# A second block product per group in the MLPs of a two-layer trunk: seven products in place of eight for all columns, alternating with the first layer

## The chip, the cores and the metric

The kernel runs on one core of a Trainium2 chip. The metric is the time of one execution on the device in microseconds (us), the median of three runs. A profiled execution is a further one, with its own time. Engines: TensorE (PE, with its weight loads PEld), VectorE (DVE), ScalarE (ACT), GpSimd (POOL), SyncE (SP). Each takes its instructions in the order in which the build wrote them.

## The reference, cut to what matters

256 tokens of width 2048 pass through two layers. Each has a recurrent mixer and a dense MLP with a hidden width of 8192, both between RMS norms, and a residual add. Only the MLP is touched:

```python
def sqrelu_mlp(h, w_up, w_down):
    u = jax.nn.relu(h @ w_up)
    return (u * u) @ w_down

f = sqrelu_mlp(rmsnorm(h, norm_mlp_pre[i]), mlp_w_up[i], mlp_w_down[i])
h = h + rmsnorm(f, norm_mlp_post[i])
```

`h` in the last line is the residual stream, 256 x 2048 in float32. Everything is float32. The kernel gets near that precision by splitting each operand into a rounded part (hi) and the rest (lo) and adding three products: hi·hi, hi·lo, lo·hi.

## The kernel before

**Splitting.** A weight block is 128 partitions x 2048 float32, 1 MiB. SP loads it into one of three `raw` tiles. It is split by halves of 1024 columns: ScalarE writes hi (`split_hi`, L103), VectorE writes lo = raw - hi (`split_lo`, L107), each into one of five buffers.

**First layer** (`up`, L526). The hidden width is taken in 8 groups of 1024, each of 8 blocks of 128. One block is one *first-layer product* (`gemmT`, L148): 16 matmuls of 512 columns (both parts of the activations against hi) and 16 of 256 (against lo), into one bank. It is folded (`fold`: ScalarE copies one half, VectorE adds), made relu and squared, and split into hi and lo of `U`.

**Second layer.** For a group, 1024 hidden rows meet 4 column blocks of 512 (n = 0 to 3) for two token tiles (t = 0, 1). In *plain* form (`plain`, L644) one column block takes 2 x 8 x 3 = 48 matmuls of 512. For n = 0, 1 the kernel treats the product as a 2 x 2 block matrix product (token tile x half of the hidden rows, times half x column block) and uses seven products in place of eight, after Strassen and Winograd (`seven`, L595). One of the seven takes 4 x 3 = 12 matmuls of 512. Four of them use sums of activation blocks, which VectorE forms (`combine`, L514); weights are summed too. Writing B11, B21 for the two halves of the hidden rows at the first column block and B12, B22 at the second, these are the weight sums:

- the *run* tile (pool `sump`, one buffer): first B11 + B12, then B22 is added, then B21. Adding is done by an accumulating DMA that POOL issues (`add_to`, L571).
- the *q* tiles (pool `accp`, two halves, one buffer): B12 + B22.

After each product VectorE adds the bank to, or takes it from, the sums `m[n, t]` (`put`, L588).

**Order.** Emission order is that of the generators `up`, `seven` and `plain`. All of a group's first-layer products are emitted, then `down` mixes the seven products of that group with the plain ones of the group before. A build-time scheduler then moves instructions somewhat, engine by engine; what it wrote is fixed.

The residual `h` lies in SBUF throughout (L55), 2 MiB.

## Time and profile before

| | |
|---|---|
| median of 3 runs | 2280.74 us (2280.22 to 2281.78) |
| profiled execution, its own time | 2281.16 us |
| its span, first to last instruction | 2279.4 us |
| mean granted TensorE clock | 0.999 |
| span of the first MLP, about | 447 to 1121 us |
| span of the second MLP, about | 1683 to 2279 us |
| HBM read | 513.47 MB |

The page gives the busy time of each engine, then groups of instructions. Matmuls overlap, so the pace of TensorE is read from the starts of its instructions. "Landing" of a DMA is the time from its issue until its data is there. The releaser in brackets is what ended an engine's idle time.

### The profile page before, as it was taken

The numbers are of one execution on the slowest core, as the hardware profiler recorded it, in microseconds if no ns is written. First come the engines' busy times: TensorE is split into PE (matmuls) and PEld (weight loads), VectorE is DVE, ScalarE is ACT, GpSimd is POOL, SyncE is SP. The second block draws the span as 40 slices with busy tenths as digits, with TensorE's granted clock in tenths as the row PEclk, the third lists the DMA queues.
The fourth block names the chain that finished last, engine by engine and source line by source line (L and its number), as shares of the span: only waits on it lengthen the run. The fifth ranks groups of instructions, "written<-read, shape, count | busy, mean of one in ns | idle before, by whom it ended". The sixth has DMA issues, their size and how long they took to land.

```text
span 2279.4 us, 30175 instructions
## 1 busy us (share of the span) xinstructions
PE 2263.6 (99%) x11528; PEld 1925.7 (84%) x11528; DVE 1719.5 (75%) x2575; ACT 1330.1 (58%) x1919; POOL 69.6 (3%) x84
## 2 busy tenths in 40 slices
PE   9999999999999999999999999999999999999998
PEld 7888888888888888888888887888888888888887
DVE  6887877667778778778786767656787877877877
ACT  7555554556555556555567456555665555555654
POOL 0000000000000000000000000000000000000000
PEclk9999999999999999999999999999999999999999
DMA  8544545558888788788764544465789878878875
GB/s 330 169 165 165 177 156 185 173 196 260 271 289 261 247 262 267 247 277 255 244 222 150 202 166 149 166 208 184 248 269 310 249 247 279 249 247 277 255 246 162
DMA packets 82288, 517.52 MB, mean 227 GB/s; under 512 B 9792, under 2 KB 10176, under 8 KB 25696
## 3 DMA queue, kind: packets, MB, share of 16 engines
q1 hardware_dynamic: 70480, 448.23, 54.2%
q0 software_dynamic: 11520, 67.11, 15.5%
q8 instruction: 90, 1.47, 0.3%
q14 instruction: 54, 0.44, 0.1%
q10 hardware_dynamic: 144, 0.26, 0.0%
HBM read 513.47 MB, written 2.10 MB: 226 GB/s over the span
## 4 chain that ended last, share of the span: by engine, by line
PE 93%; DVE 3%; DMA 2%; ACT 1%; issue 0%; SPq 0%; DVEq 0%; ACTq 0%
PE mmT L155 26%; PE mmT L158 14%; PE mm L137 12%; PE mm L136 12%; PE mm L135 12%; PE sa L620 7%; PE sb L620 3%; PE sc L620 2%; PE sc L758 2%; DVE lo L107 1%; DMA bs<-w_dn 1%; DMA raw<-w_dn 1%; PE tr L191 1%; DVE xhl L204 1%; PE sd L793 0%
## 5 line engine op out<-in xcount | busy, mean ns | idle before, releaser
L107 DVE TENSOR_TENSOR lo<-raw,hi 128x1024 fp32r<-128x1024 f32 x744 | 902.8, 1222 | 319.8 <-ACT hi L103 250.8
L103 ACT ACTIVATE hi<-raw 128x1024 fp32r<-128x1024 f32 x744 | 781.7, 1059 | 562.4 <-PE mm L137 248.2
L155 PE MATMUL mmT<-xhl,hi 128*128 128x512 f32 x2704 | 654.7, 392 | 0.0
L155 PEld LDWEIGHTS mmT<-xhl,hi 128*128 128x128 f32 x2704 | 497.2, 188 | 97.4 <-issue 1.4
L136 PE MATMUL mm<-lo,xhl 128*128 128x512 f32 (+1 forms) x1280 | 498.2, 389 | 1.4 <-DVE lo L272 1.2
L137 PE MATMUL mm<-hi,xhl 128*128 128x512 f32 x1280 | 497.3, 389 | 0.0
L135 PE MATMUL mm<-hi,xhl 128*128 128x512 f32 x1280 | 487.3, 391 | 1.3 <-ACT hi L271 0.8
L158 PEld LDWEIGHTS mmT<-xhl,lo 128*128 128x128 f32 x2704 | 347.3, 191 | 13.6 <-issue 0.5
L158 PE MATMUL mmT<-xhl,lo 128*128 128x256 f32 x2704 | 353.5, 283 | 0.0
L135 PEld LDWEIGHTS mm<-hi,xhl 128*128 128x128 f32 x1280 | 240.5, 188 | 51.5 <-ACT hi L271 2.1
L136 PEld LDWEIGHTS mm<-lo,xhl 128*128 128x128 f32 x1280 | 240.5, 188 | 50.8 <-DVE lo L272 2.7
L137 PEld LDWEIGHTS mm<-hi,xhl 128*128 128x128 f32 x1280 | 240.5, 188 | 49.2 <-issue 0.6
L103 ACT ACTIVATE hi<-bs 128x1024 fp32r<-128x1024 f32 x128 | 135.2, 1060 | 90.7 <-PE mm L137 30.5
L107 DVE TENSOR_TENSOR lo<-bs,hi 128x1024 fp32r<-128x1024 f32 x128 | 153.8, 1222 | 38.6 <-ACT hi L103 34.4
L571 POOL DMA_DIRECT2D bs<-w_dn x80 | 69.4, 868 | 2160.0 <-DMA bs<-w_dn 1149.4
L552 DVE TENSOR_TENSOR xhl<-half,xhl 128x256 fp32r<-128x256 f32 x120 | 50.7, 423 | 59.7 <-ACT half L551 59.7
L550 ACT ACTIVATE xhl<-half 128x256 fp32r<-128x256 f32 x120 | 49.3, 411 | 67.3 <-DVE half L548 67.2
L620 PE MATMUL sb<-hi,as 128*128 128x512 f32 x256 | 86.8, 390 | 0.0
L620 PE MATMUL sa<-hi,as 128*128 128x512 f32 x256 | 84.1, 389 | 0.0
L620 PE MATMUL sa<-hi,xhl 128*128 128x512 f32 x256 | 84.1, 389 | 0.0
L164 ACT COPY half<-mmT 128x256 f32<-128x256 f32 x169 | 60.9, 361 | 36.6 <-PE mmT L158 36.1
L165 DVE TENSOR_TENSOR half<-mmT,half 128x256 f32<-128x256 f32 x169 | 70.5, 418 | 0.6 <-ACT half L164 0.6
(209 smaller groups left out, 1854.8 us busy)
## 6 DMA issues: line engine op xcount, KB each, us to landing
raw<-w_up SPq DMA_DIRECT2D x128, 1024.0 KB, 7.1
raw<-w_dn SPq DMA_DIRECT2D x112, 1024.0 KB, 5.0
raw<-w_hin SPq DMA_DIRECT2D x56, 1024.0 KB, 4.9
bs<-w_dn POOLq DMA_DIRECT2D x48, 1024.0 KB, 8.8
raw<-w_gin SPq DMA_DIRECT2D x48, 1024.0 KB, 4.9
raw<-w_hout SPq DMA_DIRECT2D x16, 1024.0 KB, 4.9
bs<-w_dn SPq DMA_DIRECT2D x32, 512.0 KB, 8.2
bs<-w_dn SPq DMA_DIRECT2D x16, 1024.0 KB, 9.4
```

Source lines behind the costliest of these rows:

```text
L103: A.activation(hi, raw, AF.Copy)
L107: V.tensor_tensor(half[1], raw, half[0].bitcast(F32), ALU.subtract)
L135: PE.matmul(ps, xh, hi[:, kk, cs], start=(k == 0), stop=False)
L136: PE.matmul(ps, xh, lo[:, kk, cs], start=False, stop=False)
L137: PE.matmul(ps, xl, hi[:, kk, cs], start=False, stop=(k == nk - 1))
L155: PE.matmul(ps, hi, X.both(k), start=(k == 0), stop=False)
L158: PE.matmul(ps[:, 0, :], lo, X.both(k)[:, 0, :], start=False, stop=(k == KT - 1))
L164: A.copy(u, ps[:, 1, :])
L165: V.tensor_tensor(u, ps[:, 0, :], u, ALU.add)
L552: V.tensor_tensor(lo, u, hi.bitcast(F32), ALU.subtract)
L571: nc.gpsimd.dma_start(raw, b, accum_op=ALU.add)
L620: PE.matmul(bank[b], l, r[:, kk, :], start=first and j + kk + i == 0, stop=j + kk + i == 4, skip_group_check=not first)
```

## The change

It leaves every result the same up to rounding and does five things.

1. In groups 0 to 5 of both MLPs, `seven` is used for columns n = 2, 3 as well. A group there has two *pairs* of column blocks, p = 0 and 1; groups 6 and 7 keep plain products for n = 2, 3.
2. The products are emitted between the first-layer products of the next group: a table `plan` says which after each. For a group with both pairs it is, with G a first-layer product and the numbers those of `seven`: G 7' 1 2, G 3 4, G 5, G 6, G 7 1 2, G 3 4, G 5, G 6. 7' belongs to the pair before.
3. The seven products stand in another order: 1 (B11), 2 (B21), 3 (run = B11 + B12), 4 (B22), 5 (run with B22), 6 (q = B12 + B22), 7 (run with B21). VectorE forms B11 + B12 with two adds of 1024 columns (L655) from the raw tile of B11 and from q, which holds B12 by then; after that POOL accumulates B22 into q. So a pair has three accumulated blocks (four before) and four plain loads from `w_dn` (five before, and four for each plain pair).
4. Two first-layer blocks are made relu, squared and split together (512 columns, `relu_squared`), and `combine` uses fewer and wider instructions.
5. The activation sums of even groups use the room of the residual. `h` is written to DRAM at the start of the MLP and read back after the last first-layer product. Banks for the products come from the pools `pssc` and `pstr`.

```diff
+    residue = []
+    def hs(t, c):
+        return residue[-1][:, t, c]
+    def new_residue():
+        residue.append(hpool.tile([P, NT, D], F32, tag="h", name=nm("h")))
...
         def sums_of_a(g):
+            if g % 2 == 0:
+                four = hpool.tile([P, HK, 2, 4, P], F32R, tag="h", name=nm("as")) if g == 0 else sa[0]
+                return [four[:, j] for j in range(HK)] if g == 0 else four
             two = featp.tile([P, 2, 2, 4, P], F32R, tag="qk", name=nm("as"))
...
+        def relu_squared(g, u, js):
+            n = len(js)
+            V.scalar_tensor_tensor(u, u, 0.0, bc(rr[0].unsqueeze(1), [P, n, T]), ALU.max, ALU.mult)
+            hi, lo = (uT[g].t[0][:, js[0]:js[-1] + 1:HK, part, :] for part in range(2))
+            A.activation(hi, u, AF.Square)
+            A.activation(u, u, AF.Square)
+            V.tensor_tensor(lo, u, hi.bitcast(F32), ALU.subtract)
...
+        def up(g):
+            for i in range(HK):
+                u = tok().rearrange("p (a n) -> p a n", a=2)
+                unfold(gemmT(w_up, g * GK + i, X), u[:, 0, :])
+                yield
+                if i == 0:
+                    uT[g] = Xhl(GK)
+                    sa[g] = sums_of_a(g)
+                unfold(gemmT(w_up, g * GK + HK + i, X), u[:, 1, :])
+                relu_squared(g, u, [i, HK + i])
+                yield
+                b = u.rearrange("p a (t n) -> p (a t) n", t=NT)
+                combine(sa[g][i], b[:, 0, :], b[:, 2, :], b[:, 1, :], b[:, 3, :], b[:, 1:3, :])
...
+        def load_b12(g, p):
+            b12.append([accp.tile([P, 1024], F32, tag=tag, name=nm("bs")) for tag in ("accA", "accB")])
             for j in range(2):
-                nc.sync.dma_start(sums["Q"][j], block(g, 0, 1)[:, j, :])
-                add_to(sums["Q"][j], block(g, 1, 1)[:, j, :])
+                nc.sync.dma_start(b12[-1][j], block(g, 0, 2 * p + 1)[:, j, :])
...
-            run = sums["run"], sums["tile"]
-            product("b", summed(0), run[0], 1, 0)
-            add_to(run[1], block(g, 1, 1))
-            product("a", pure(1, 0), raw_of(0, 0), 0, 1)
+            b11 = raw_of(0, n0)
+            product("a", pure(1, 0), b11, n0, 1)
             yield
-            product("c", pure(1, 1), raw_of(1, 0), 0, 1)
-            product("b", summed(3), raw_of(1, 1), 1, 1)
-            product("a", summed(2), run[0], 1, 1, -1)
-            add_to(run[1], block(g, 1, 0))
+            product("c", pure(1, 1), raw_of(1, n0), n0, 1)
             yield
-            product("a", summed(1), sums["Q"], 1, 0, -1)
-            if g < NG - 1:
-                begin_q(g + 1)
+            tile_ = sump.tile([P, 2, 1024], F32, tag="run", name=nm("bs"))
+            run, q = [tile_[:, j, :] for j in range(2)], b12.pop(0)
+            for j in range(2):
+                V.tensor_tensor(run[j], b11[j], q[j], ALU.add)
+            for j in range(2):
+                add_to(q[j], block(g, 1, n1)[:, j, :])
+            product("b", summed(S), run, n1, 0, -1)
+            add_to(tile_, block(g, 1, n1))
             yield
-            product("a", pure(0, 1), run[0], 0, 0)
-            if g < NG - 1:
-                begin_run(g + 1)
+            product("b", summed(S3), raw_of(1, n1), n1, 1, -1)
+            yield
+            product("a", summed(S5), run, n1, 1, -1)
+            add_to(tile_, block(g, 1, n0))
+            yield
+            product("a", summed(R), q, n1, 0, -1)
+            if following is not None:
+                load_b12(*following)
+            yield
+            product("a", pure(0, 1), run, n0, 0)
+            yield
...
+        both = (0, 1, 2, 3, 4, 5)
+        LAST = NG - 1
+        order = [(g, p) for g in range(NG) for p in range(2 if g in both else 1)]
...
+        spill = aside.tile([P, NT, D], F32, tag="h", name=nm("aside"))
+        nc.sync.dma_start(spill, residue[-1])
...
+        for g in range(1, NG):
...
+            if g - 1 in both:
+                b = it[g - 1, 1]
+                plan = [[*late, a, a], [a, a], [a], [a], [a, b, b], [b, b], [b], [b]]
+            elif g < LAST:
+                plan = [[*late, a, a], [a, n2], [a, n2], [a], [n3, a], [n3], [a], []]
+            else:
+                plan = [[*late, a, a], [a], [a], [a], [a], [a], [], []]
+            for what in plan:
+                next(u)
+                step(*what)
+            next(u, None)
+        new_residue()
+        nc.sync.dma_start(residue[-1], spill)
+        a = it[LAST, 0]
+        step(n2, a, a, a, n2, a, n3, a, n3, a)
```

How the built order moves, at three places inside the first MLP. `bs` is the run tile or a half of q, `raw` a plain block, `mmT` the bank of a first-layer product, `sa`, `sb`, `sc` the banks of block products, `as` the summed activations, `xhl` activations.

VectorE, from the second split of the run tile to the next split of the same tile. Before (the run tile is `bs_5271`):

```order
L107 TENSOR_TENSOR lo_5634<-bs_5271,hi_5633 128x1024
L593 TENSOR_TENSOR tok_5000<-tok_5000,sc_5578 128x512
L107 TENSOR_TENSOR lo_5650<-raw_5647,hi_5649 128x1024
L107 TENSOR_TENSOR lo_5654<-raw_5647,hi_5653 128x1024
L593 TENSOR_TENSOR tok_5098<-tok_5098,sb_5491 128x512
L107 TENSOR_TENSOR lo_5682<-bs_5193,hi_5681 128x1024
L107 TENSOR_TENSOR lo_5692<-bs_5194,hi_5691 128x1024
L593 TENSOR_TENSOR tok_5098<-tok_5098,sa_5516 128x512
L107 TENSOR_TENSOR lo_5711<-raw_5708,hi_5710 128x1024
L107 TENSOR_TENSOR lo_5715<-raw_5708,hi_5714 128x1024
L107 TENSOR_TENSOR lo_5747<-bs_5271,hi_5746 128x1024
```

In the changed kernel, from product 3 to product 5 (the run tile is `bs_6883`):

```order
L117 TENSOR_TENSOR lo_6900<-bs_6883,hi_6899 128x1024
L542 TENSOR_TENSOR as_6457<-tok_6711,as_6457 128x512
L615 TENSOR_TENSOR tok_5307<-tok_5307,sc_6811 128x512
L117 TENSOR_TENSOR lo_6914<-raw_6911,hi_6913 128x1024
L117 TENSOR_TENSOR lo_6924<-raw_6911,hi_6923 128x1024
L117 TENSOR_TENSOR lo_6945<-raw_6942,hi_6944 128x1024
L558 TENSOR_TENSOR tok_6717<-mmT_6833,half_6876 128x256
L117 TENSOR_TENSOR lo_6949<-raw_6942,hi_6948 128x1024
L615 TENSOR_TENSOR tok_5409<-tok_5409,sb_6888 128x512
L549 SCALAR_TENSOR_TENSOR tok_6717<-tok_6717,rr_4609 128x512
L117 TENSOR_TENSOR lo_6988<-bs_6883,hi_6987 128x1024
L553 TENSOR_TENSOR xhl_6456<-tok_6717,xhl_6456 128x2x256
```

Between the two splits of the tile there were six other splits and three puts; now there are four splits, two puts and three smaller ones. The second split for product 5 stands behind the low half of the squares (L553).

VectorE, at the end of a run tile. Before, its last split is followed by other work, and the next tile is filled by DMA alone:

```order
L107 TENSOR_TENSOR lo_5747<-bs_5271,hi_5746 128x1024
L107 TENSOR_TENSOR lo_5757<-bs_5271,hi_5756 128x1024
L593 TENSOR_TENSOR tok_4974<-tok_4974,sa_5516 128x512
L107 TENSOR_TENSOR lo_5775<-raw_5772,hi_5774 128x1024
L107 TENSOR_TENSOR lo_5779<-raw_5772,hi_5778 128x1024
```

In the changed kernel (`bs_7080` is a half of q, `bs_7257` the next pair's run tile):

```order
L117 TENSOR_TENSOR lo_7070<-bs_6708,hi_7069 128x1024
L615 TENSOR_TENSOR tok_5434<-tok_5434,sa_6787 128x512
L117 TENSOR_TENSOR lo_7095<-raw_7092,hi_7094 128x1024
L117 TENSOR_TENSOR lo_7099<-raw_7092,hi_7098 128x1024
L117 TENSOR_TENSOR lo_7138<-bs_6883,hi_7137 128x1024
L558 TENSOR_TENSOR tok_6940<-mmT_7009,half_7052 128x256
L549 SCALAR_TENSOR_TENSOR tok_6940<-tok_6940,rr_4609 128x512
L117 TENSOR_TENSOR lo_7148<-bs_6883,hi_7147 128x1024
L615 TENSOR_TENSOR tok_5409<-tok_5409,sa_6787 128x512
L655 TENSOR_TENSOR bs_7257<-raw_7158,bs_7080 128x1024
```

The adds for the next run tile now follow the last split of the old one with one put between them, and everything behind them on VectorE waits with them.

TensorE, at the first matmul of product 5. Before:

```order
L620 MATMUL sb_5491<-hi_5602,as_5274 128x512
L620 MATMUL sb_5491<-hi_5612,as_5275 128x512
L620 MATMUL sa_5516<-hi_5623,as_5274 128x512
L620 MATMUL sb_5491<-lo_5613,as_5275 128x512
L620 MATMUL sb_5491<-hi_5612,as_5275 128x512
```

In the changed kernel:

```order
L168 MATMUL mmT_6191<-xhl_4267,lo_6195 128x256 x8
L643 MATMUL sa_6037<-hi_6237,as_4953 128x512
L168 MATMUL mmT_6191<-xhl_4268,lo_6199 128x256 x4
L643 MATMUL sb_6138<-hi_6163,as_4953 128x512
L643 MATMUL sb_6138<-lo_6164,as_4953 128x512
L643 MATMUL sb_6138<-hi_6163,as_4953 128x512 x2
```

The first matmul of product 5 (`hi_6237` is a split of the run tile with B22) stood in the middle of product 4; now it stands ahead of all of product 4 and inside a first-layer product.

More of the change, by code (lines that the diff above doesn't have):

```diff
@@ L651, in plain @@
                         mm_half(ps[t], half, 2 * c + j, uT[g], t, GK)
-            for t in range(NT):
-                put(n, t, ps[t])
-        def down(g):
-            two, three, steps = plain(g, 2), plain(g, 3), seven(g + 1)
-            next(two)
-            next(two)
-            next(steps)
-            next(two, None)
-            next(steps)
-            next(three)
-            next(three)
-            next(steps)
-            next(three, None)
-            next(steps, None)
-        def rest(it):
-            for _ in it:
-                pass
@@ L673, in mlp @@
[L673 to L689 removed]
+                if c:
+                    for t in range(NT):
+                        put(n, t, ps[t])
@@ new lines, in plain, with step @@
+                yield
+        both = (0, 1, 2, 3, 4, 5)
+        LAST = NG - 1
+        order = [(g, p) for g in range(NG) for p in range(2 if g in both else 1)]
+        it = {}
+        for i, (g, p) in enumerate(order):
+            it[g, p] = seven(g, p, order[i + 1] if i + 1 < len(order) else None)
+        def step(*what):
+            for w in what:
+                next(w)
+        spill = aside.tile([P, NT, D], F32, tag="h", name=nm("aside"))
+        nc.sync.dma_start(spill, residue[-1])
@@ L690, in mlp @@
+        new_residue()
+        nc.sync.dma_start(residue[-1], spill)
+        a = it[LAST, 0]
+        step(n2, a, a, a, n2, a, n3, a, n3, a)
+        g = LAST
+        n2 = plain(g, 2)
+        for t, n in ((0, 1), (1, 0), (1, 1)):
+            post.take(m[n, t], n, t)
         if ahead is not None:
             ahead.split(2)
-        rest(plain(g, 2))
+        step(n2, a)
+        post.take(m[0, 0], 0, 0)
         if ahead is not None:
-            ahead.split(3)
+            ahead.split(1)
@@ L695, in mlp @@
+        step(n2)
+        if ahead is not None:
+            ahead.split(2)
         post.wp(3)
```

131 lines of the change are left out of this document (54 added, 77 removed).

## Prediction

> **What bounds the kernel now.** I read the page first, then the windows of one group of eight first-layer blocks, then the rows of single instructions in that group.
>
> ```profile
> PE 2263.6 (99%) x11528; PEld 1925.7 (84%) x11528; DVE 1719.5 (75%) x2575; ACT 1330.1 (58%) x1919; POOL 69.6 (3%) x84
> PE 93%; DVE 3%; DMA 2%; ACT 1%; issue 0%; SPq 0%; DVEq 0%; ACTq 0%
> q1 hardware_dynamic: 70480, 448.23, 54.2%
> q0 software_dynamic: 11520, 67.11, 15.5%
> core 0: us, PE busy (x) PEld busy (x) DVE busy (x) ACT busy (x) POOL busy (x), PEclk, DMA share, GB/s
> 447.00:1121.00 674.00, 673.02 (x3430) 574.40 (x3429) 515.71 (x750) 400.20 (x575) 33.05 (x38) 1.00 0.81 256
> 952.25:1037.59 85.34, 85.34 (x438) 73.16 (x437) 66.28 (x95) 49.92 (x66) 4.36 (x6) 1.00 0.83 259
> ```
>
> TensorE is busy 99% of the span and makes 93% of the chain of waits. In the window of one group (85.34 us) it has no gap. VectorE needs 66.3 us of it, the DMA engines 83%. So work taken from TensorE comes off the time until something else needs more than TensorE has left. The matmul pace shows in starts, not in the 389 ns of one, since matmuls overlap:
>
> ```profile
> 475.45 0.39 PE L136 MATMUL mm<-lo,xhl 128*128 128x512 f32 x1
> ...
> 485.88 0.39 PE L137 MATMUL mm<-hi,xhl 128*128 128x512 f32 x1
> 1082.96 3.82 PE L155 MATMUL mmT<-xhl,hi 128*128 128x512 f32 x16
> 1086.62 2.08 PE L158 MATMUL mmT<-xhl,lo 128*128 128x256 f32 x16
> 1088.53 3.82 PE L155 MATMUL mmT<-xhl,hi 128*128 128x512 f32 x16
> ```
>
> 46 matmuls of 512 lie between the first two rows: 10.43 / 46 = 0.2267 us each. A first-layer product takes 1088.53 - 1082.96 = 5.57 us. A group before is 8 of those (44.6), 84 matmuls of block products (19.0) and 96 plain ones (21.8), together 85.4, as the window says.
>
> **What the change removes.** In six groups of each MLP the plain pair of columns (96 matmuls) becomes seven products of 12 (84). That is 12 x 12 = 144 matmuls x 0.2267 = 32.6 us, all on TensorE. A group then holds two equal "pairs" of four first-layer products and seven block products: 4 x 5.57 + 84 x 0.2267 = 41.3 us a pair on TensorE, where half a group now takes 42.7.
>
> **What it adds to VectorE and DMA.** VectorE's pitch, start to start:
>
> ```profile
> 790.76 1.23 DVE L107 TENSOR_TENSOR lo<-raw,hi 128x1024 fp32r<-128x1024 f32 x1 [0.43 <-ACT hi L103]
> 791.90 0.68 DVE L593 TENSOR_TENSOR tok<-tok,sa 128x512 f32<-128x512 f32 x1
> 792.50 1.22 DVE L107 TENSOR_TENSOR lo<-raw,hi 128x1024 fp32r<-128x1024 f32 x1
> 752.95 0.42 DVE L165 TENSOR_TENSOR half<-mmT,half 128x256 f32<-128x256 f32 x1
> 753.40 0.43 DVE L548 SCALAR_TENSOR_TENSOR half<-half,rr 128x256 f32<-128x256 f32 x1
> 758.10 0.42 DVE L165 TENSOR_TENSOR half<-mmT,half 128x256 f32<-128x256 f32 x1
> 758.44 0.68 DVE L522 TENSOR_TENSOR as<-tok,as 128x512 fp32r<-128x512 f32 x1
> 755.42 0.29 DVE L519 TENSOR_TENSOR tok<-tok,half 128x128 f32<-128x128 f32 x1
> 755.63 1.22 DVE L107 TENSOR_TENSOR lo<-raw,hi 128x1024 fp32r<-128x1024 f32 x1
> ```
>
> So 1.14 us for 1024 columns, 0.60 for 512, 0.34 for 256 (0.45 if the next one reads it), 0.20 for 128. A pair holds 22 splits and the two adds that form B11+B12 (24 x 1.14 = 27.4), 7 puts (4.2), 4 unfoldings (1.4) and two rounds of squaring and combining (5.1): 38.1 us, under 41.3. Had each its full duration (1.22 and so on), it would be 42.0.
>
> DMA: q1 takes 0.542 x 2279.4 / 448.23 = 2.76 us per MB, 2.89 for a 1 MiB block; q0, the accumulating queue, 5.52. Before, a group has 17 blocks on q1 and 4 on q0: 71.2 us, 83% of 85.34, as measured. After, 16 and 6: 79.3, so 39.7 a pair against 41.3. No engine alone is over TensorE, but all three are over 92% of it, and what decides is the order of waits between them.
>
> **The ring.** The run tile exists once, and so does its companion q. From pair to pair it goes round: the adds write it, product 3 splits it, B22 is accumulated into it, product 5 splits it, B21 is accumulated, product 7 splits it, and only then come the next adds. The same link stands in the trace of before:
>
> ```profile
> 798.54 2.36 DVE L107 TENSOR_TENSOR lo<-bs,hi 128x1024 fp32r<-128x1024 f32 x2
> 801.19 0.86 POOL L571 DMA_DIRECT2D bs<-w_dn  x1 [18.74 <-DVE lo L107]
> 810.84 1.06 ACT L103 ACTIVATE hi<-bs 128x1024 fp32r<-128x1024 f32 x1 [1.75 <-DMA bs<-w_dn]
> 811.93 1.23 DVE L107 TENSOR_TENSOR lo<-bs,hi 128x1024 fp32r<-128x1024 f32 x1 [1.59 <-ACT hi L103]
> 793.97 2.01 ACT L103 ACTIVATE hi<-raw 128x1024 fp32r<-128x1024 f32 x2 [1.89 <-PE sb L620]
> L521 ACT ACTIVATE as<-tok 128x512 fp32r<-128x512 f32 x64 | 39.7, 624 | 27.5 <-DVE tok L520 27.4
> bs<-w_dn POOLq DMA_DIRECT2D x1, 1024.0 KB, 9.5
> ```
>
> The second split ends at 800.90, POOL issues 0.3 later, the block lands after 9.5, ScalarE starts 0.15 later, VectorE 1.1 after that: 11.0 us from split to split, and ScalarE and VectorE both waited in it. Before, the ring ran once in 85 us, so this cost TensorE nothing. After, it runs twice. With L1 and L2 for the landings of B22 and B21, and VectorE's instructions as the build orders them:
> - From the adds to the end of product 3's second split VectorE issues 10 of 1024, 3 of 512, 2 of 256, 2 of 128: 9 x 1.14 + 1.22 + 1.8 + 0.7 + 0.4 = 14.4.
> - 0.45 + L1, then to the end of product 5's second split: two ScalarE splits (2.0), two squares of 512 queued behind them (1.1), 0.1, and on VectorE 0.60 + 0.34 + 1.22 = 5.4. VectorE's second split stands behind the low half of the squares, which waits for both.
> - 0.45 + L2, then 1.1 + 1.14 + 0.45 + 0.60 + 1.14 + 0.60 = 5.0 to the next adds.
>
> Ring: **25.7 + L1 + L2**. VectorE has 8 us of other work under L1 and about 9 under L2, so landings below about 6.4 and 8.1 gain nothing. The reload of q is nearly as late: product 6's second split ends 6.7 us after product 5's, and a half block takes 8.2 (row below), so the second add could start 15.1 after; the run path gives 14.2 + 1.1 at L2 = 8.7.
>
> The landings:
>
> ```profile
> bs<-w_dn POOLq DMA_DIRECT2D x48, 1024.0 KB, 8.8
> bs<-w_dn SPq DMA_DIRECT2D x32, 512.0 KB, 8.2
> bs<-w_dn POOLq DMA_DIRECT2D x1, 1024.0 KB, 7.9
> 816.14 0.86 POOL L571 DMA_DIRECT2D bs<-w_dn  x1 [0.44 <-issue]
> 825.14 0.86 POOL L571 DMA_DIRECT2D bs<-w_dn  x1 [8.13 <-DMA bs<-w_dn]
> bs<-w_dn POOLq DMA_DIRECT2D x1, 1024.0 KB, 12.9
> ```
>
> The shortest I found is 7.9 (issued at 781.59, in a stretch of first-layer loads), the median 8.8, the block of 801.19 took 9.5, and one issued 9.0 us behind two half blocks for q (825.14) took 12.9, that is 21.9 after the second of them. After the change B22 is issued 12 us behind q's second half: 21.9 - 12 = 9.9 if the queue drains no faster. I take L1 = 9.5, the lower of that and of the block of 801.19, and for L2, with an empty queue ahead of it, 8.7, next to the median. Ring: 43.9 us. That is 2.6 over TensorE's 41.3, and TensorE loses it at product 5's first matmul, which the build puts ahead of product 4's: product 4 queues behind that wait.
>
> By the Trainium skill, "DMA: Bandwidth & Descriptors", the section on the anatomy of one DMA on the SWDGE path, such a transfer takes about 2.0 us plus its bytes at 436 GB/s; for 1 MiB that is an estimate of 4.4. The trace disagrees for these accumulations: 8.8. By 4.4 the ring would be 40.2 (VectorE's own work under both links) and TensorE would bound.
>
> **The rest.** The residual goes to DRAM once per MLP (2 MiB) while the ring has not yet started: no cost. Its reload (2 MiB, about 5.8 us of q1) stands between blocks that the tail waits for; between 0 and 6 us per MLP, I take 1 each since the DMA engines are over 80% busy but three blocks are loaded ahead. If that cover is gone it is 12 in all. Fewer, wider squarings on ScalarE cost nothing, as it is 58% busy.
>
> **Sum.** 12 pairs per MLP close the ring 11.5 times (the first starts early, the last is followed by a single pair with eight first-layer products): 23 rings x 2.6 = 59.8. So -32.6 + 59.8 + 2 = +29 us on a span of 2279.4: 2308.6. The profiled execution took 2281.16, 1.76 more than its span, and is 0.4 over the median of the runs: **2310**.
>
> **Rivals.**
> - *The landings are short, and TensorE bounds again.* For it: 7.9 is what before shows beside first-layer loads, and after the change first-layer loads are spread over the whole group. Against: DMA demand is 96% of TensorE's time. With both at 7.9 and VectorE's floor of 8.1 the ring is 41.7: -32.6 + 23 x 0.4 + 2 = -21, 2260; at 8.4 each 42.5, 2278. VectorE at full durations (42.0) would give 2266. The chance of a gain in this way is 0.22, and 0.05 more that the ring never binds (2250).
> - *It comes out even.* L1 + L2 near 17.0 gives a ring of 42.7: 0.08. A change under 0.2% (4.6 us) is not told from none here.
> - *The accumulating queue falls behind for good.* If q's two halves delay B22 as they delayed the block of 825.14, L1 = 12.9 and with L2 = 8.8 the ring is 47.4, TensorE idles 6.1 us each time: 2279 + 111 = 2390. From L1 + L2 = 20 on (45.7, 2350) I count it here. Against: a longer ring empties the queue. 0.12.
> - The change does what it says: the build has 144 matmuls of 512 fewer.
>
> **Numbers.** The forecast (ring 43.0 to 45.2, so 2290 to 2340) has 0.53. Slower in all 0.65, even 0.08, faster 0.27. The range goes down to 2258, which holds nearly all of the first rival with a binding ring, and up to 2345, leaving some 0.05 below and 0.12 above.
>
> **What would show it.** Right: about one TensorE gap of 2 to 4 us per pair, ahead of a product-5 matmul, released by ScalarE, which itself waited for the accumulated block; POOL's two issues to one run tile 14 to 17 us apart; a group period near 88 us. The matmul step is right if the count falls by 144 and the pace stays 0.227. Wrong: a period of 82.6 to 85 us with TensorE at 99%, or gaps released by VectorE with no DMA wait behind them (then VectorE's sum was short), or by plain loads (then DMA bandwidth). A landing median of B22 and B21 under 8.3 would make the forecast fall.

## The result, and the profile after

| | before | after |
|---|---|---|
| median | 2281.26 us (2280.22 to 2282.39, 4 runs) | 2343.41 us (2337.37 to 2347.96, 4 runs) |
| profiled execution, its span | 2279.4 us | 2346.2 us |
| mean granted TensorE clock | 0.999 | 0.988 |

Ratio 1.0271, 95% interval 1.0247 to 1.0295: 62 us slower. The forecast was 2310, 29 us slower. The direction came out and so did the mechanism, a ring with an accumulated block in it; the size was half.

The page of the changed kernel: busy time by engine, queues, and the chain of waits by engine and line.

```profile
PE 2261.8 (96%) x11384; PEld 1918.1 (82%) x11384; DVE 1854.5 (79%) x2571; ACT 1384.7 (59%) x1879; POOL 97.2 (4%) x116
q1 hardware_dynamic: 70480, 439.84, 49.9%
q0 software_dynamic: 16128, 88.09, 20.6%
PE 67%; DMA 15%; DVE 12%; ACT 3%; issue 2%; SPq 0%; DVEq 0%; ACTq 0%; POOLq 0%
bs<-w_dn POOLq DMA_DIRECT2D x56, 1024.0 KB, 9.5
```

The 144 matmuls are gone (11528 to 11384), yet TensorE falls from 99% to 96% of a longer span, and from 93% to 67% of the chain. The DMA wait that took its place is the block accumulated into the run tile. The waits, totals over the span (us, times, longest):

```profile
ACT hi L113 <- DMA bs<-w_dn: 204.8, 43, 8.3
PE sa L643 <- ACT hi L113: 66.0, 24, 4.8
```

The first of them before:

```profile
ACT hi L103 <- DMA bs<-w_dn: 18.3, 7, 4.8
```

ScalarE waits 205 us for accumulated blocks (18.3 before). TensorE has 24 gaps, as many as there are pairs in the groups that have two, in front of a block product and released by ScalarE; they are 2.75 us long on average.

One pair of the first MLP, a lap of the ring, start to start of the adds. First VectorE and ScalarE, then POOL, then TensorE:

```profile
724.89 2.35 DVE L655 TENSOR_TENSOR bs<-raw,bs 128x1024 f32<-128x1024 f32 x2
736.85 2.35 DVE L117 TENSOR_TENSOR lo<-bs,hi 128x1024 fp32r<-128x1024 f32 x2
750.24 2.00 ACT L113 ACTIVATE hi<-bs 128x1024 fp32r<-128x1024 f32 x2 [7.75 <-DMA bs<-w_dn]
751.32 1.23 DVE L117 TENSOR_TENSOR lo<-bs,hi 128x1024 fp32r<-128x1024 f32 x1 [4.85 <-ACT hi L113]
753.46 0.69 DVE L553 TENSOR_TENSOR xhl<-tok,xhl 128x512 fp32r<-128x512 f32 x1 [0.91 <-ACT tok L552]
754.40 1.22 DVE L117 TENSOR_TENSOR lo<-bs,hi 128x1024 fp32r<-128x1024 f32 x1
764.98 1.06 ACT L113 ACTIVATE hi<-bs 128x1024 fp32r<-128x1024 f32 x1 [2.35 <-DMA bs<-w_dn]
770.01 1.22 DVE L655 TENSOR_TENSOR bs<-raw,bs 128x1024 f32<-128x1024 f32 x1
...
727.78 0.86 POOL L601 DMA_DIRECT2D bs<-w_dn  x1 [0.27 <-ACT half L557]
739.50 0.86 POOL L601 DMA_DIRECT2D bs<-w_dn  x1 [10.86 <-DVE lo L117]
756.15 0.86 POOL L601 DMA_DIRECT2D bs<-w_dn  x1 [15.79 <-DVE tok L539]
...
751.34 0.50 PE L643 MATMUL sa<-hi,as 128*128 128x512 f32 x1 [4.02 <-ACT hi L113]
```

The adds at 724.89; product 3's second split done at 739.20; B22 issued at 739.50; ScalarE can split at 750.24; VectorE's second split of product 5 done at 755.62; B21 issued at 756.15, split from 764.98; the next adds at 770.01. So 14.3, 0.3 + 10.7, 5.4, 0.5 + 8.8, 5.0: 45.1 us with what the rounding leaves. (POOL's row at 727.78 is q's second half; it comes up below.) Under the first link (the time from issue to split) VectorE runs out of work and stands 4.85 + 0.91 us; under the second only a fraction. TensorE stands 4.02 us at product 5's first matmul, its only gap in the lap.

A mean lap, from VectorE's adds of the second and the twelfth pair of the first MLP:

```profile
589.70 2.35 DVE L655 TENSOR_TENSOR bs<-raw,bs 128x1024 f32<-128x1024 f32 x2
1042.32 2.35 DVE L655 TENSOR_TENSOR bs<-raw,bs 128x1024 f32<-128x1024 f32 x2
```

452.62 / 10 = 45.26 us; the second MLP gives 45.68 in the same way. TensorE's work is 41.3.

### The profile page after: what moved, and what is told of

The parts are those of the page before. It is cut to its first block, busy times and chain, and to the rows that moved or that the text cites. A ratio compares the mean times of both kernels' runs of the same rounds, so it can differ in the third digit from the quotient of the medians.

```text
span 2346.2 us, 30156 instructions
## 1 busy us (share of the span) xinstructions
PE 2261.8 (96%) x11384; PEld 1918.1 (82%) x11384; DVE 1854.5 (79%) x2571; ACT 1384.7 (59%) x1879; POOL 97.2 (4%) x116
## 4 chain that ended last, share of the span: by engine, by line
PE 67%; DMA 15%; DVE 12%; ACT 3%; issue 2%; SPq 0%; DVEq 0%; ACTq 0%; POOLq 0%
PE mmT L165 17%; DMA bs<-w_dn 12%; PE mmT L168 10%; PE mm L145 8%; PE mm L147 8%; PE mm L146 8%; DVE lo L117 7%; PE sa L643 7%; PE sb L643 4%; DMA raw<-w_dn 2%; PE sc L804 2%; ACT hi L113 2%; DVE tok L615 1%; PE sc L643 1%; PE tr L201 1%
## 5 line engine op out<-in xcount | busy, mean ns | idle before, releaser
L117 DVE TENSOR_TENSOR lo<-raw,hi 128x1024 fp32r<-128x1024 f32 x720 | 867.8, 1221 | 199.6 <-ACT hi L113 135.9
L113 ACT ACTIVATE hi<-bs 128x1024 fp32r<-128x1024 f32 x224 | 234.8, 1059 | 273.9 <-DMA bs<-w_dn 204.8
L117 DVE TENSOR_TENSOR lo<-bs,hi 128x1024 fp32r<-128x1024 f32 x224 | 270.9, 1220 | 135.8 <-ACT hi L113 135.4
L146 PE MATMUL mm<-lo,xhl 128*128 128x512 f32 (+1 forms) x896 | 348.9, 389 | 2.3 <-DVE lo L283 1.2
L145 PE MATMUL mm<-hi,xhl 128*128 128x512 f32 (+1 forms) x896 | 347.8, 391 | 2.3 <-ACT hi L282 1.8
L147 PE MATMUL mm<-hi,xhl 128*128 128x512 f32 (+1 forms) x896 | 348.0, 389 | 0.0
L145 PEld LDWEIGHTS mm<-hi,xhl 128*128 128x128 f32 x896 | 168.4, 188 | 37.9 <-ACT hi L282 3.4
L147 PEld LDWEIGHTS mm<-hi,xhl 128*128 128x128 f32 x896 | 168.3, 188 | 34.4 <-issue 0.6
L643 PE MATMUL sb<-hi,as 128*128 128x512 f32 x448 | 160.8, 422 | 0.0
L643 PEld LDWEIGHTS sa<-hi,as 128*128 128x128 f32 x448 | 84.8, 189 | 86.1 <-ACT hi L113 70.9
L643 PEld LDWEIGHTS sb<-hi,as 128*128 128x128 f32 x448 | 94.0, 210 | 19.9
L643 PEld LDWEIGHTS sa<-hi,xhl 128*128 128x128 f32 x448 | 84.2, 188 | 16.9
L643 PE MATMUL sb<-lo,as 128*128 128x512 f32 x224 | 94.9, 424 | 0.0
```

Of the source, the lines that this page charges most:

```text
L113: A.activation(hi, raw, AF.Copy)
L117: V.tensor_tensor(half[1], raw, half[0].bitcast(F32), ALU.subtract)
L145: PE.matmul(ps, xh, hi[:, kk, cs], start=(k == 0), stop=False)
L146: PE.matmul(ps, xh, lo[:, kk, cs], start=False, stop=False)
L147: PE.matmul(ps, xl, hi[:, kk, cs], start=False, stop=(k == nk - 1))
L643: PE.matmul(bank[b], l, r[:, kk, :], start=first and j + kk + i == 0, stop=j + kk + i == 4, skip_group_check=not first)
```

## The experiments

The theory: a lap is set by VectorE's fixed order with two links in it, each 0.45 + landing + 1.1 us; what a lap loses is the part of a link that VectorE has no other work for. The rivals: the amount of VectorE work, the amount of DMA, or one of the other edits.

**The second pairs alone.** Undone: all other edits stay.

```diff
-        both = (0, 1, 2, 3, 4, 5)
+        both = ()
```

> No group has a second pair (plain products for n = 2, 3 everywhere); the rest of the change stays: the new order of the seven products, the two adds on VectorE, the wider squaring, the spill and reload of the residual, the interleaving. Theory: the ring runs once per 85 us and is slack, so 2275 to 2290, like the kernel before (2281). Rival 3 (the loss lies in one of the other edits): 2300 to 2345. Rivals 1 and 2: near 2281 too.

2282.13 us, ratio 1.0005 (0.9996 to 1.0014). The new order, the adds by VectorE, the wide squarings and the residual's trip to DRAM together cost nothing that can be told from none (at most 3 us). The loss is in the second pairs.

**No accumulation into the run tile.** Left out are B22 and B21 in the sums, so products 5 and 7 use B11 + B12. VectorE's instructions and their order are the same.

```diff
-            add_to(tile_, block(g, 1, n1))
...
-            add_to(tile_, block(g, 1, n0))
```

> The two accumulations into the run tile (B22, then B21) are left out, so products 5 and 7 use wrong weights; all splits, adds, matmuls and VectorE's order stay. Theory: with no landing in it the ring falls under TensorE's 41.3 us per pair, so the 144 matmuls saved come through: 2248 to 2262. Rival 1 (VectorE): its 38 us and its waits for ScalarE stay, so above 2300. Rival 2 (DMA bandwidth, here relieved by 11 of 39.7 us per pair) also says a gain, to 2250 to 2300; the next run tells it from the theory.

2250.63 us, ratio 0.9867 (0.9852 to 0.9881). A lap is 41.23 us in both MLPs, TensorE's 41.3 as summed in the prediction.

```profile
PE 2232.6 (99%) x11384; PEld 1900.8 (85%) x11384; DVE 1858.7 (83%) x2571; ACT 1396.5 (62%) x1879; POOL 48.8 (2%) x60
```

VectorE does as much as after (1858.7 us), and TensorE is at 99%. So VectorE's amount is not it: the accumulations are. Whether as bytes or as a link this run does not tell.

**The same bytes elsewhere.** Two runs keep the two accumulations but take them out of the ring. In the first they go to blocks in DRAM, in the second into q; either way the products get other sums.

```diff
-            add_to(tile_, block(g, 1, n1))
+            add_aside(block(g, 1, n1))
```

> The same two accumulations per pair, of the same bytes from HBM, go into scratch tiles in DRAM that nobody reads, in place of the run tile; products 5 and 7 use wrong weights. The DMA engines keep their load, nothing waits for it. Theory: as without the accumulations, 2248 to 2265. Rival 2 (bandwidth): the load of 39.7 us per pair stays, so it stays near 2343, at least above 2310. Rival 1: above 2300.

2380.26 us, ratio 1.0433 (1.0416 to 1.0451). It tells nothing of the ring: with no reader to hold them, the build put all of these DMAs at the start of the program, and the loss is there. In the MLPs a lap was 41.2.

```diff
-            for j in range(2):
-                add_to(q[j], block(g, 1, n1)[:, j, :])
+            for n in (n1, n1, n0):
+                for j in range(2):
+                    add_to(q[j], block(g, 1, n)[:, j, :])
...
-            add_to(tile_, block(g, 1, n1))
...
-            add_to(tile_, block(g, 1, n0))
```

> The accumulations of B22 and B21 are again left out of the run tile, but the same 2 MiB per pair are accumulated into q behind its own B22, in SBUF and on the same queue, so that the DMA engines carry as much as in the changed kernel (39.7 us per pair); products 5, 6 and 7 use wrong weights. Product 6 reads q late, some 30 us after the adds, so this chain has room. Theory (only landings between two uses of the run tile count): 2248 to 2270. Rival 2 (DMA bandwidth as such): above 2310. (The run with scratch tiles in DRAM told nothing on this: the scheduler moved all of those accumulations to the start of the program.)

2284.89 us, ratio 1.0016 (1.0007 to 1.0025), a lap of 43.0. Neither account had this. With the run tile out of the link 58 of the 62 us are back, so bytes alone don't cost them. But a lap is still 1.7 over TensorE's: the one TensorE gap of a lap I read (2.13 us at 827.11) had ScalarE waiting 3.06 us for a plain w_up block. Over the whole run ScalarE waits 146.5 us for plain blocks of the MLPs (74.5 for `w_up`, 72.0 for `w_dn`; 7.3 and 38.0 in the changed kernel), so all these bytes within one stretch of the lap seem to make plain blocks late. It still waits 69.3 us for accumulated ones.

**Taking one landing away.** VectorE adds B22 from the raw tile of product 4 in place of the DMA.

```diff
-            add_to(tile_, block(g, 1, n1))
-            product("b", summed(S3), raw_of(1, n1), n1, 1, -1)
+            b22 = raw_of(1, n1)
+            product("b", summed(S3), b22, n1, 1, -1)
+            for j in range(2):
+                V.tensor_tensor(run[j], run[j], b22[j], ALU.add)
```

> B22 is added to the run tile by VectorE, from the raw tile that product 4 loads anyway, and not by an accumulating DMA. Nothing else is changed and the output stays. The ring loses the landing of 10.8 us and gets two adds (2.3); VectorE's work rises from 38.1 to 40.4 us per pair, DMA's falls to 34.2. Theory: the ring is about 36 us and no longer binds; VectorE with its short waits for ScalarE needs 41.5 to 42.7 against TensorE's 41.3: 2255 to 2285, under the kernel before or equal to it. Rival 1 (VectorE's amount of work bounds the changed kernel): VectorE gets more, so slower than the changed kernel, above 2345.

2297.29 us, ratio 1.0071 (1.0056 to 1.0086), a lap of 43.3: 46 better than after, 12 worse than the worse end expected. The waits of the run, and one of VectorE in a lap:

```profile
ACT hi L113 <- DMA bs<-w_dn: 42.4, 15, 4.3
PE sa L643 <- DVE tok L615: 29.1, 24, 1.2
760.98 1.23 DVE L117 TENSOR_TENSOR lo<-bs,hi 128x1024 fp32r<-128x1024 f32 x1 [2.20 <-PE sa L643]
```

The DMA wait is mostly gone (204.8 to 42.4). VectorE has 40.4 us of work and waits 0.72 + 2.20 more in a lap, for buffers that TensorE releases; TensorE waits 24 times for a bank that VectorE empties. Two engines at over 93% with fixed orders wait for each other in turn, and I had left that out. That it sets the lap here is read from these waits, not tried alone.

GpSimd instead of VectorE for the same adds (`G.tensor_tensor` in the last line above):

> As with VectorE adding B22, but GpSimd does the two adds of 1024 columns, so VectorE keeps 38.1 us per pair. No trace here shows how long GpSimd takes for one. Theory: up to about 5 us each the ring stays under 41.3 and the time is 2250 to 2270; at 10 us each the ring is as long as in the changed kernel, 2340 or more. Its adds also stand ahead of the next accumulations on GpSimd's queue.

2303.09 us, ratio 1.0099 (1.0082 to 1.0116). GpSimd's adds, and VectorE's splits beside them (mean 1360 ns; 1221 in the changed kernel, in its row in the last section):

```profile
L663 POOL TENSOR_TENSOR bs<-bs,raw 128x1024 f32<-128x1024 f32 x56 | 198.4, 3560 | 301.9 <-DVE lo L117 166.3
L117 DVE TENSOR_TENSOR lo<-raw,hi 128x1024 fp32r<-128x1024 f32 x720 | 967.0, 1360 | 172.7 <-ACT hi L113 126.4
PE mmT L168 <- DVE lo L117: 25.8, 22, 1.4
```

The two adds of a pair take 7 us on GpSimd, and VectorE's splits from raw tiles take 99 us more in all. It is the adds that do it: the 86 splits that run beside one of them take 2401 ns on average, the other 876 take 1219. TensorE now waits for VectorE.

Accumulating in halves, so that a split can start on the first:

```diff
-            add_to(tile_, block(g, 1, n1))
+            for j in range(2):
+                add_to(run[j], block(g, 1, n1)[:, j, :])
```

(and the same for B21)

> Each accumulation into the run tile is issued as two halves of 1024 columns, so each split waits for its own half alone. Bytes, splits and VectorE's order stay. Theory: the first half goes out 1.1 us earlier and lands after about 6; the second lands about when the whole block did. Behind B22 the ring gains 1 to 2 us, behind B21 2 to 3: about 41.3 to 42.3, and 2250 to 2278. Rivals 1 and 2: no gain, about 2343, or more for the extra issues.

2313.38 us, ratio 1.0142 (1.0127 to 1.0157). In one lap the halves of B22 landed after 9.0 and 12.9 us, the second later than the whole block did (10.7). ScalarE, in order, then waits twice:

```profile
875.66 1.06 ACT L113 ACTIVATE hi<-bs 128x1024 fp32r<-128x1024 f32 x1 [4.09 <-DMA bs<-w_dn]
880.67 1.06 ACT L113 ACTIVATE hi<-bs 128x1024 fp32r<-128x1024 f32 x1 [3.95 <-DMA bs<-w_dn]
```

**Order alone.** The same instructions and bytes, another table. I added up what VectorE's order holds between a tile's splits, with the durations of the prediction: in the changed kernel 7.3 us of other work under the first link and 9.4 under the second. With the landings measured the links need 0.45 + 10.7 + 1.1 = 12.2 and 10.5.

```diff
-                plan = [[*late, a, a], [a, a], [a], [a], [a, b, b], [b, b], [b], [b]]
+                plan = [[*late, a, a, a], [a], [a], [a], [a, b, b, b], [b], [b], [b]]
```

> Only the table of the order: product 3 goes ahead of the second first-layer product, so the numbers are G 7' 1 2 3, G 4, G 5, G 6. VectorE's other work is 9.2 us under the first link (7.3 in the changed kernel) and 10.3 under the second (9.4). Theory: each lap is shorter by 1.9 + 0.9, so 45.3 - 2.8 = 42.5, and 23 x 2.8 = 64 off 2343: 2275 to 2295. Rival (amounts of DMA or VectorE work): above 2320.

2284.77 us, ratio 1.0008 (0.9999 to 1.0018); the expected 42.5 a lap came out at 42.8 and 43.0. Moving one product of each pair by one place takes back 59 of 62 us. In a lap:

```profile
825.31 2.01 ACT L113 ACTIVATE hi<-bs 128x1024 fp32r<-128x1024 f32 x2 [3.89 <-DMA bs<-w_dn]
826.40 1.23 DVE L117 TENSOR_TENSOR lo<-bs,hi 128x1024 fp32r<-128x1024 f32 x1 [2.86 <-ACT hi L113]
826.42 0.50 PE L643 MATMUL sa<-hi,as 128*128 128x512 f32 x1 [0.86 <-ACT hi L113]
PE sa L643 <- ACT hi L113: 20.8, 17, 2.5
```

VectorE's wait under the first link is 2.86, TensorE's gap 0.86. The theory gave 12.2 - 9.2 = 3.0 with the landing of the changed kernel; this block landed after 11.3 (11.2 on average in this order), which would give 3.6.

**Orders that cover both links.** The rest went the other way. Products 1 and 2 ahead of 7', and 5 and 6 later:

```diff
+                plan = [[a, a, *late, a], [a], [], [a, a], [b, b, a, b], [b], [], [b, b]]
```

> Only the table of the order is changed; the same 11384 matmuls, the same bytes, the same accumulations into the run tile. Products 1 and 2 of the next pair go ahead of product 7 of the pair before, and products 5 and 6 go one first-layer product later. By VectorE's durations of the trace of before (1.14, 0.60, 0.34, 0.20 us) VectorE then has 10.7 us of other work between product 3's second split and product 5's first (7.3 in the changed kernel), and 13.9 between product 5's second and product 7's first (9.4). Theory (what costs is the time that VectorE, in its fixed order, stands in the two links 0.45 + landing + 1.1, 12.2 and 10.5 us with the landings measured): VectorE's wait falls from 4.9 + 1.1 to 1.5 + 0, a lap comes near TensorE's 41.3, and the time is 2250 to 2268, faster than before. Rival (the amounts: DMA engines over 90% busy, or VectorE's own 38.1 us with full durations): the amounts are the same, so the time stays near 2343, above 2320.

2366.13 us, ratio 1.0373 (1.0358 to 1.0389). The same with 5 and 6 where they were:

```diff
+                plan = [[a, a, *late, a], [a], [a], [a], [b, b, a, b], [b], [b], [b]]
```

> Only the table of the order: products 1 and 2 of the next pair ahead of product 7 of the pair before, product 3 ahead of the second first-layer product, 5 and 6 where they were. VectorE's other work is 7.4 us under the first link, as in the changed kernel (7.3), and 17.6 under the second (9.4). Theory: only the second wait, 1.1 us, goes; a lap of 44.2 and 2343 - 23 x 1.1 = 2318, so 2305 to 2330. If the place of the products mattered as such (the distance between 5 and 7, or the blocks held longer), it would be as fast as the order that helps both links, under 2270; if amounts, 2343.

2409.71 us, ratio 1.0559 (1.0542 to 1.0577). With product 1 alone ahead of 7':

```diff
+                plan = [[a, *late, a, a], [a], [a], [a], [b, a, b, b], [b], [b], [b]]
```

> Order alone: G 1 7' 2 3, G 4, G 5, G 6, with 5 ahead of 6 as in the changed kernel. It differs from the order G 7' 1 2 3, G 4, G 5, G 6 (2285) in product 1 alone. VectorE's other work is 9.6 us under the first link (9.2 there) and 13.5 under the second (10.3 there, 10.5 needed). Theory: only 0.2 + 0.4 of waits to gain, so 2270 to 2285. If the raw tile that B11 holds one product longer is what made the other orders slow, it is above 2300.

2351.03 us, ratio 1.0301 (1.0284 to 1.0318). I had blamed the raw tile of B11, held until the adds. A fourth raw tile tests that, in the first of these orders and, as control, in the good one:

```diff
-    wraw = ctx.enter_context(tc.tile_pool(name="wraw", bufs=3))
+    wraw = ctx.enter_context(tc.tile_pool(name="wraw", bufs=4))
-    tokp = ctx.enter_context(tc.tile_pool(name="tok", bufs=12))
-    halfp = ctx.enter_context(tc.tile_pool(name="half", bufs=6))
+    tokp = ctx.enter_context(tc.tile_pool(name="tok", bufs=10))
+    halfp = ctx.enter_context(tc.tile_pool(name="half", bufs=2))
```

> The order that covers both links (products 1 and 2 of the next pair ahead of 7, products 5 and 6 one first-layer product later; 2366 with three raw tiles) with a fourth raw tile; the room comes from two fewer of the 512-column tiles (10 for 12) and four fewer of the 256-column ones (2 for 6). VectorE's other work: 11.6 us under the first link, 13.9 under the second. If the raw tile that B11 holds until the adds was what made that order slow (ScalarE waited 178 us for w_up blocks), those waits go and TensorE bounds near 41.3: 2250 to 2285. If it was the place of the adds (ScalarE waited 4.9 us for them in one lap and TensorE 3.6 behind it), it stays above 2320.

> The order G 7' 1 2 3, G 4, G 5, G 6 (2285) with the same fourth raw tile and the same smaller pools: the control for the run beside it. Theory: the raw tile is not short there; the first link keeps 12.2 - 9.6 = 2.6 us of wait, and only ScalarE's waits for plain loads (79 us in all, mostly under that wait) go: 2268 to 2288. If a third plain block in flight slows the accumulated ones, the landing of B22 rises over 11.2 and the time over 2290.

2356.96 us, ratio 1.0326 (1.0312 to 1.0340), 9 better than with three; control 2287.51 us, ratio 1.0024 (1.0014 to 1.0034). The raw tile is not the main cause. What these orders share stands on POOL. With four raw tiles, the first of q's halves, the second, and B22, and what ScalarE waited for it:

```profile
782.65 0.86 POOL L601 DMA_DIRECT2D bs<-w_dn  x1 [18.92 <-DVE bs L655]
783.79 0.86 POOL L601 DMA_DIRECT2D bs<-w_dn  x1 [0.27 <-issue]
787.02 0.86 POOL L601 DMA_DIRECT2D bs<-w_dn  x1 [2.37 <-DVE lo L117]
802.03 1.06 ACT L113 ACTIVATE hi<-bs 128x1024 fp32r<-128x1024 f32 x1 [4.25 <-DMA bs<-w_dn]
```

Product 3's splits follow the adds at once, so B22 is issued 3.2 us behind q's second half (11.7 after the change) and lands only after 14.9 us (mean over the pairs 14.5, 14.6, 14.8 and 14.5 in the four kernels so far with products ahead of 7'; 10.7 after the change). The link is now 0.45 + 14.9 + 1.1 = 16.4 against 11.6 us of work, which leaves 4.9 to wait, as the changed kernel has (12.2 - 7.3); the laps are alike too (45.6 and 45.5). I had held the landing fixed while moving its issue. In this lap q's second half lands at 794.5, 7.5 us after B22 was issued behind it; in the changed kernel it had landed before B22 was issued in every pair. That the queue sets this landing is read from such times, not isolated in a run of its own. The order that took 2409.71, with 7.4 us of work under the first link, fits: 0.45 + 14.6 + 1.1 - 7.4 = 8.8 us of wait there is 3.9 more than in the changed kernel. Less the 1.1 saved under the second link that is 2.8 a lap, and 23 x 2.8 = 64; it is 66 slower.

Two more orders. Products 5 and 6 later without the rest:

```diff
+                plan = [[*late, a, a, a], [a], [], [a, a], [a, b, b, b], [b], [], [b, b]]
```

> Order alone: G 7' 1 2 3, G 4, G, G 5 6. B11 is held no longer than in the changed kernel. VectorE's other work is 12.8 us under the first link (12.2 needed) and 7.4 under the second (10.5 needed). Theory: 3.1 us of wait a lap in place of 6.0, lap 42.4: 2268 to 2288, no clear gain over the order with 5 and 6 earlier (2285), as the wait only changes links. Rival (another tile becomes the bound): above 2300.

2416.43 us, ratio 1.0580 (1.0565 to 1.0594), a lap of 48.5. In a lap VectorE waits 3.04 us for B21, as worked out (3.1), and none for B22. But other waits have come:

```profile
SPq L608 <- DVE tok L558: 147.8, 26, 6.2
ACT hi L113 <- DMA raw<-w_up: 114.3, 41, 5.7
PE sa L643 <- DVE lo L117: 62.4, 48, 2.1
```

SP waits at L608 for q, which a later product 6 releases later (147.8 + 35.3 us in two rows; 10.1 + 68.3 after the change), and first-layer loads stand behind it on SP; ScalarE waits 114 us for them. That one causes the other is my reading; it was not tried alone. Product 6 ahead of 5, which adds into the same bank in the order 5, 6 and so leaves other sums here:

```diff
+                plan = [[a, *late, a, a], [a], [a, a], [], [b, a, b, b], [b], [b, b], []]
```

> Order alone again. Within a pair product 6 (which needs q, not the run tile) goes ahead of product 5; product 1 of the next pair goes ahead of product 7 of the pair before, product 2 stays behind it: G 1 7' 2 3, G 4, G 6 5, G. VectorE's other work is 12.7 us under the first link (12.2 by the landings measured in the changed kernel) and 9.6 under the second (10.5). The adds stand 7.8 us of VectorE's work ahead of the end of product 3's splits (14.3 in the changed kernel, 10.3 where product 3 was only moved ahead of a first-layer product, 5.8 where both links were covered and the time rose to 2366). Theory: both waits go but 1 us, B11's raw tile is released one product later than in the changed kernel and not two, so TensorE bounds a lap at 41.3 to 42.3: 2250 to 2275. Rival (the wait only moves on: ScalarE's split of the run tile behind late adds, and loads of first-layer blocks behind the raw tile that B11 holds): above 2290, with ScalarE waiting for the adds or for plain loads.

2388.68 us, ratio 1.0466 (1.0450 to 1.0481): the expected rival, again with product 1 ahead of 7'. ScalarE waits 87.9 us for `w_up` blocks and 62.0 for those of `w_dn`, but only 28.5 for accumulated ones, so here the landings of B22 and B21 can hardly set the lap. What makes the plain blocks late was not tried.

**The good order and VectorE's adds together** (the two diffs above in one kernel).

> The order G 7' 1 2 3, G 4, G 5, G 6 with B22 added by VectorE from the raw tile that product 4 loads anyway (two adds of 1024 columns, 2.3 us more a pair: 40.4 of 41.3), so the first link has no landing and the second has 9.7 to 10.3 us of VectorE's other work for 10.5. Theory: a lap of 41.3 to 42.3 with VectorE at over 95% of it: 2255 to 2280. If the raw tile of B22, held until its adds, or VectorE's own work is the bound, a lap of 43 and more, as in the order of the changed kernel with the same adds (43.3; 2297): 2285 to 2300.

2290.71 us, ratio 1.0039 (1.0026 to 1.0051), laps of 41.4 and 43.9 in turn. Above the expected 2280; as with the same adds in the first order, VectorE and TensorE wait for each other (PE's weight loads 19.7 us for VectorE's puts, VectorE 26.5 for TensorE).

**Why B22 lands in 10.7 us.** Two kernels move B22's accumulation ahead of q's halves. In the first the build put POOL's order back to that of the changed kernel, so it is only a repeat:

```diff
-            for j in range(2):
-                add_to(q[j], block(g, 1, n1)[:, j, :])
             product("b", summed(S), run, n1, 0, -1)
             add_to(tile_, block(g, 1, n1))
+            for j in range(2):
+                add_to(q[j], block(g, 1, n1)[:, j, :])
```

> The accumulations of B22 into q are issued behind that of B22 into the run tile, not ahead of it; nothing is added or removed, and VectorE's order stays as it is. Theory (the ring of the run tile: 25.7 us + two landings, 45.3 us per pair now, of which B22 lands after 10.8 and B21 after 8.9): B22 no longer queues behind q's halves and lands after about 8.6, B21 after 9 to 9.5, so the ring is about 43.8 to 44.2 and the time 2305 to 2318, against 2343. Rival 1 (VectorE has too much work) and rival 2 (DMA bandwidth): the work is the same, so no change, 2338 to 2348. Rival 3 (the loss lies in the spill, the tail or the new order around them): no change.

2348.36 us, ratio 1.0289 (1.0268 to 1.0309). In the second POOL's order is written out:

```diff
+            with tc.manual_schedule(engines={mybir.EngineType.Pool}):
+                add_to(tile_, block(g, 1, n1))
+                for j in range(2):
+                    add_to(q[j], block(g, 1, n1)[:, j, :])
```

> POOL issues the accumulation of B22 ahead of the two halves of q, in a fixed order. What it tells apart is the cause of B22's landing of 10.7 us (8.7 for B21, on the same queue). If B22 stands behind q's halves in the accumulating queue, it now lands in 8.7 or less, a lap is 2 us shorter and the time about 2300. If it shares the DMA engines with the two plain blocks of 1 MiB that are loaded in the same microseconds (the trace shows all 16 engines busy, half of it the plain queue), it still takes 10 or more and the time stays 2335 to 2355.

2349.91 us, ratio 1.0303 (1.0288 to 1.0318). Half of each account: B22 lands in 8.6 on average, and the lap is no shorter, since B21, now the next behind q, takes 11.5; it is issued before q's second half has landed.

In the changed kernel no queue was ahead of B22. In the lap shown q's second half was issued at 727.78 and landed after 7.5, at 735.3, and B22 was issued at 739.50; in all 28 pairs q had landed first. What fits these runs is the plain traffic beside a block. In the changed kernel, the windows of B22 and of B21 in one lap (columns as in the windows of before: the last three are clock, DMA share, GB/s), and what the queues moved in B22's (MB, share) and then in B21's:

```profile
739.50:750.20 10.70, 7.82 (x41) 6.50 (x39) 6.97 (x9) 2.38 (x3) 0.86 (x1) 1.00 1.00 305
756.15:764.85 8.70, 8.70 (x49) 7.54 (x48) 8.19 (x11) 4.93 (x6) 0.86 (x1) 1.00 0.83 196
...
q1 hardware_dynamic: 298, 2.20, 49.1%
q0 software_dynamic: 144, 1.05, 50.7%
...
q0 software_dynamic: 144, 1.05, 65.3%
q1 hardware_dynamic: 80, 0.66, 18.1%
```

Both windows accumulate 1.05 MB. With 2.20 MB of plain loads beside it the block takes 10.7, with 0.66 it takes 8.7; in the next two laps 1.59 MB gave 9.4 and 2.52 gave 11.5. That is (11.5 - 8.7) / (2.52 - 0.66) = 1.5 us for each MB beside it. In the run with B22 ahead of q, 0.71 MB ran beside a B22: 8.7. All 56 accumulated blocks of the changed kernel lie along such a line (correlation 0.95). A longer landing also counts more MB; but with the MB of the first 8 us alone the two still go together (0.83). VectorE's work does not order the landings: in the two windows it was busy 6.97 us of the longer and 8.19 of the shorter. So this is well supported, but no run moved the plain loads alone. By the Trainium skill, "DMA: Bandwidth & Descriptors", the section on queues, rings and completion order, each DMA engine takes the queues that have work in turn, a packet at a time. That both queues have half of the engines' time in B22's window (49% and 51%) fits; the counts, 298 packets to 144, are not one for one, and no run here tests the rule.

**All runs by one sum.** The run without accumulation has a lap of 41.2 and takes 2250.6. With 23 laps, the time of any other kernel with the second pairs should be 2250.6 + 23 x (lap - 41.23), but for the one that accumulates in DRAM. Laps are the means of both MLPs, measured as above:

| kernel | lap | sum | measured |
|---|---|---|---|
| product 3 earlier, four raw tiles | 42.6 | 2283 | 2287.5 |
| product 3 earlier, VectorE's adds | 42.8 | 2286 | 2290.7 |
| product 3 earlier | 42.9 | 2289 | 2284.8 |
| accumulations into q | 43.0 | 2291 | 2284.9 |
| B22 by VectorE | 43.3 | 2298 | 2297.3 |
| B22 by GpSimd | 43.5 | 2302 | 2303.1 |
| halves | 44.3 | 2321 | 2313.4 |
| B22 ahead of q | 45.3 | 2345 | 2349.9 |
| the change | 45.5 | 2348 | 2343.4 |
| the change, repeat | 45.6 | 2350 | 2348.4 |
| both links covered, four raw tiles | 45.6 | 2350 | 2357.0 |
| both links covered | 46.1 | 2362 | 2366.1 |
| product 1 ahead of 7' | 46.1 | 2362 | 2351.0 |
| 6 ahead of 5 | 47.5 | 2395 | 2388.7 |
| 5 and 6 later | 48.5 | 2418 | 2416.4 |
| both links covered, 5 and 6 as they were | 48.8 | 2424 | 2409.7 |

The sum is within 7 us of the time in all but three (8, 11 and 15). So the time is the lap, whichever wait sets it. No kernel that has the second pairs and does all of their work got under 2281: the best, product 3 earlier, is level with before. The 2250.6 that TensorE allows stays out of reach by these means.

## Why the prediction was right and wrong

- **The matmuls removed: right.** 144 fewer, and with no accumulation the lap is 41.23 us (41.3 predicted) and the kernel 30.5 us under before (32.6 - 2 predicted).
- **VectorE's work: right in amount.** A lap of the changed kernel holds 38.3 us of it (38.1 predicted); with full amounts and no landing it stays hidden.
- **DMA's amount: not the bound by itself.** The bytes put elsewhere left 1.7 us of the 4.2 that a lap loses, mostly as late plain blocks.
- **The ring's fixed part: right.** 14.3 + 0.3 + 5.4 + 0.5 + 5.0 = 25.5 (25.7 predicted), with the gap where it was said to be: TensorE at product 5's first matmul, released by ScalarE, which waited for the accumulated block; one per pair.
- **The landing of B22: the step that failed.** I took L1 = 9.5, the landing of the block of 801.19, as the lower of that and 21.9 - 12 = 9.9, the queue's carry-over. It measured 10.7 (26 pairs, 8.4 to 11.7), and L2 9.0 for 8.7. That is 1.5 us a lap; 23 x 1.5 = 34.5, about the whole miss of 33. The carry-over was not there, as q had landed before B22 was issued. What I missed is what runs beside: I spread first-layer loads over the group in words and did not count the 2.2 MB of plain loads, of `w_up` and `w_dn`, that fall into B22's 10.7 us. The trace of before had it: 1.40 MB ran beside the block of 801.19 (9.5), 0.28 beside the shortest (7.9). That the traffic is the reason stays an inference, as said above. Both landings lay inside the bounds I had (7.9 to 12.9), and the rival of a queue that falls behind began at a sum of 20.0; 19.7 was measured.
- **The other edits and the reload of the residual: about 1 us,** which is told neither from none nor from the 2 us allowed.
- **The rivals of short landings and of an even result: wrong.** No landing of B22 came under 8.4 us.
- **What would show it:** the gaps and their releasers were as listed, POOL's two issues are 16.65 us apart in the lap shown (14 to 17), and a group of two laps is 90.5 and 91.4 us (88). That the mean gap of 2.75 us is so near the predicted 2.6 is luck: a lap lost 4.2, and the rest went into slower matmuls (last section).

## What to carry to other kernels

A buffer that exists once and is filled in place makes a ring: add its links, and compare with the work of the busiest engine for the same stretch. What a link costs is its length less the work that stands inside it in the order of the in-order engine that meets it; one product moved was worth 59 us here, and moving more was worth less than nothing, since a landing is no constant: it grows with the plain traffic beside it and with the nearness of the transfer ahead in its queue. So work out the landing again for each order, from the bytes in its own window.
